# A hybrid encoder step: the sample's place in the order of layer 0's attention tiles

## The chip, the cores and the metric

The kernel runs on one core of a Trainium2 chip. The metric is the device time of one execution in microseconds, taken as the median of several runs. A core has a matrix engine (TensorE, PE in the profile, with its weight loads as PEld), three engines for elementwise work (VectorE, DVE; ScalarE, ACT; GpSimd, POOL), and a queue engine (SyncE, SP) that here only issues DMAs. Each engine executes its instructions in order; semaphores make it wait for others. DMAs are issued from the queues of SP, POOL and ACT.

## What is computed

One inference step of a two-layer encoder, for a prompt of 2048 tokens and a sample group of 32 tokens that share the weights. Layer 0 joins a pooling mixer and a sliding-window attention, layer 1 is a forgetting attention. Cut to layer 0's attention, with q, k, v and the gate from one input projection:

```python
def sink_attention(q, k, v, bias, sinks):
    s = einsum('...qgrd,...kgd->...grqk', q, k) * ATTN_SCALE + bias
    m = maximum(max(s), sink)
    p = exp(s - m)
    w = p / (sum(p) + exp(sink - m))
    return einsum('...grqk,...kgd->...qgrd', w, v)
# prompt: 64-token chunks see themselves and the two chunks before
# sample: 32 tokens see 128 cached keys and their own 32
mixed = concatenate([pool_out, attn]) * silu(gate)
x = x + mixed @ w_out          # for the prompt and for the sample alike
```

Neither group reads anything of the other's, so their order is free.

## The kernel before

The kernel is written in Tile: pools hand out buffers by tag, instructions get their semaphores from a scheduler that also interleaves independent work on each engine. It runs five stages one after another: layer 0's input projection and pooling mixer (which writes q, k, v, the gates and the mixer's values to DRAM), layer 0's attention and output projection, layer 1's input projection with the sample's forgetting attention, the prompt's forgetting attention, and the output projection of layer 1.

Products of fp32 precision are made from exact high and low parts, so an output projection of a 128-token tile takes 8 blocks of the contraction times 3 products times 2 halves, 48 products of 512 columns (L577), and the sample's takes 32, because its high and low parts are stacked in one operand (L582).

The change touches the second stage. It handles 17 token tiles: 16 of the prompt (0 to 15, 128 tokens each) and the sample (number NT = 16, 32 tokens). Each goes through five steps, and the steps of successive tiles are staggered: in turn n the loop calls the load of the n-th tile in `order`, the scores of the one before it, the values of the one before that, then the output projection and the norm of the two before those.

- `stage_load` loads a prompt tile's keys (kk, L623 and L625), values (v2, L627) and queries (qs, L629) by DMAs of POOL's queue, with three buffers for keys and queries. For the sample it loads nothing: keys, values and queries (kabs, v2s, qss) have been prepared in SBUF at the end of stage one.
- `stage_scores` makes two products per head (L653, L654) into one of two PSUM buffers (ps), the bias and the minimum on DVE (L655), the exponential on ACT (L658), and the normalization on DVE (L665).
- `stage_values` loads the gates (sg, L671) and the mixer's values (mp, L673, one buffer) on SP's queue, splits mp into high and low parts on POOL (L157, L158; the first half of the output projection's contraction), transposes the probabilities (L690), multiplies them with the values (L694, L695), joins the halves (L699 to L702), gates on POOL (L703) and splits the result on ACT and DVE (the second half of the contraction).
- `stage_out` loads the residual on SP's queue and calls `out_proj`; for the sample that takes two copies on ACT (L586) and two additions on POOL (L587) besides.
- `stage_norm` makes layer 1's normalized input, transposes it (L725) and stores it.

In turn 2 the eight blocks of the output weights are loaded, four on POOL's queue and four on SP's (L564), and split on ACT and DVE. Turns 0 to 2 get a higher scheduling priority. The order of the tiles is one line, with the sample at the front:

```python
order = [NT] + list(range(NT))
```

SBUF of the first stage is handed to the second buffer by buffer, so most loads of the second stage can begin only when the last products of the first have read their operands. The buffers of one tag are taken in the order in which the code asks for them.

Of the kernel before, what the change touches and what calls it, by code (L numbers as in the profile page):

```python
# [17 lines left out]
P = 128  # L18
# [24 lines left out]
def hybrid_step_kernel(ctx: ExitStack, tc: tile.TileContext, *args):  # L43
# [93 lines left out]
    def rstd_bits(ss, np_, count):  # L137
        """as rstd_of, for one column and without a table: a first guess from the exponent's bits, then Newton"""
# [26 lines left out]
    def flush(n=0):  # L165
        """issue the stores that wait, but for the last n"""
        while len(pending) > n:
            dst, src, eng = pending.pop(0)
            eng.dma_start(dst, src)

    # ------------------------------------------------------------------
    # one layer's input projection, h^T held as exact hi/lo parts
    # ------------------------------------------------------------------
    class Proj:
# [13 lines left out]
        def at(self, which, tok, n):  # L188
            """hi (0) or lo (1) part of h^T for tokens [tok, tok + n): [P, KT, n]"""
# [59 lines left out]
        def prefetch(self, plan, fast=False):  # L249
            """the column groups in the order of use; the next one's weights are loaded ahead"""  # L250
# [49 lines left out]
        def turns(self, new=None):  # L300
            """the turn that waits, one step behind the arithmetic it needs"""
            for f in self.late:
                f()
            self.late = [new] if new else []

        def head_norm(self, src, np_, nh, gB, eng):
            """src: [np, nh, 64] (PSUM or SBUF) -> normalized, scaled tile [np, nh, 64]"""
# [13 lines left out]
    def turn(pt, ev, o, t0, h0, npair, dstT):  # L321
        """normalized heads [P, 2 token tiles, npair x 2 heads x 64] -> exact hi / lo parts, transposed"""
# [11 lines left out]
    # ------------------------------------------------------------------  # L334
    # layer 0, input projection and pooling mixer
    # ------------------------------------------------------------------
    smp_es = ExitStack()

    with ExitStack() as es:
# [91 lines left out]
        # ALiBi with the chunk mask, keys = 128 before the tile and its own 128  # L431
# [11 lines left out]
        # the sample's keys, values and queries for the sliding window, hi / lo parts  # L443
# [114 lines left out]
    # ------------------------------------------------------------------  # L558
    # output projection weights, as exact hi/lo parts
    # ------------------------------------------------------------------  # L560
# [6 lines left out]
    def out_proj(pp, pool, lhs, wo, xres, dst, n, eng):  # L567
        """lhs: for 128 tokens (hi, lo) APs [P, KT, 128]; for the sample one AP [P, KT, 64]"""
# [22 lines left out]
    # ------------------------------------------------------------------  # L591
    # layer 0, sliding-window attention and output projection
    # ------------------------------------------------------------------
    with ExitStack() as es:
# [136 lines left out]
        order = [NT] + list(range(NT))  # L731
# [17 lines left out]
    # ------------------------------------------------------------------  # L749
    # layer 1, input projection  # L750
    # ------------------------------------------------------------------
    late = ctx.enter_context(pool_of(name="late", bufs=1))
    mhs = late.tile([P, KT, 2 * NS], F32R, name="mhs", tag="mhs")
    with ExitStack() as es:
# [38 lines left out]
        # log forget gates and their running sums  # L793
        with pool_of(name="lf", bufs=1) as lf:
# [28 lines left out]
            def running_sums(src_h, nt, dst, tag):  # L823
                """src_h: [P, 16, nt] with positions t*128+p; dst: DRAM [16*nt, 128]"""
# [63 lines left out]
        # forgetting attention of the sample group, one pair of heads  # L888
# [11 lines left out]
        def sample_pair(hp):  # L900
            """generator: both heads side by side, the queries block diagonal"""
# [70 lines left out]
        for gc in range(4):  # L972
            if gc:
                whi, wlo = pj.next_weights()
            for tch in range(NTC):
                for cc in range(2):
# [3 lines left out]
                    # twice the gate, x * (1 + tanh(x / 2)); the half comes in with the softmax's sums  # L980
# [20 lines left out]
    # ------------------------------------------------------------------  # L1001
    # layer 1, forgetting attention over the prompt
    # ------------------------------------------------------------------
# [252 lines left out]
```

## Time and profile before

| | |
|---|---|
| time, median of 3 runs | 2679.44 us (2678.52 to 2679.57) |
| profiled execution, first to last instruction (span) | 2675.6 us |
| profiled execution, its own time outside the span | not shown |
| PE busy | 2586.7 us, 97% |
| DVE busy | 1604.6 us, 60% |
| ACT busy | 1166.4 us, 44% |
| POOL busy | 1149.9 us, 43% |
| DMA, whole span | 126 GB/s in the mean |

The profile is one execution. Its page gives sums over the span and a picture in 40 slices; the trace behind it gives single instructions with start, length, the idle time before them and what ended it. An instruction's length overlaps with its successor's on PE, so the spacing of starts is what a product costs in a full stretch. The granted clock is the share of TensorE's full 2.4 GHz that it got; 0.50 is 1.2 GHz. The attention stage runs from about 480 to about 817 us of the span.

### The profile page before, as it was taken

The numbers are of one execution on the slowest core, as the hardware profiler recorded it, in microseconds if no ns is written. First come the engines' busy times: TensorE is split into PE (matmuls) and PEld (weight loads), VectorE is DVE, ScalarE is ACT, GpSimd is POOL, SyncE is SP. The second block draws the span as 40 slices with busy tenths as digits, with TensorE's granted clock in tenths as the row PEclk, the third lists the DMA queues.
The fourth block names the chain that finished last, engine by engine and source line by source line (L and its number), as shares of the span: only waits on it lengthen the run. The fifth ranks groups of instructions, "written<-read, shape, count | busy, mean of one in ns | idle before, by whom it ended". The sixth has DMA issues, their size and how long they took to land. (4 is left out here: it accounts for less than half of the span.)

```text
span 2675.6 us, 47345 instructions
## 1 busy us (share of the span) xinstructions
PE 2586.7 (97%) x17259; PEld 2345.5 (88%) x17259; DVE 1604.6 (60%) x3847; ACT 1166.4 (44%) x2424; POOL 1149.9 (43%) x1583
## 2 busy tenths in 40 slices
PE   6999999799998999999999999999999999999999
PEld 6999999688887999999999998887888878877787
DVE  7650244778765115554553324889988988888521
ACT  5321111556554122222222114777777777777310
POOL 4454240455534434554554422555555555553100
PEclk9999999799998999999999999999999999999999
DMA  6342110976738443445555316544354455443642
GB/s 187 101 110 88 44 47 23 211 185 169 181 100 266 161 159 97 105 111 132 144 146 139 94 62 162 145 113 122 97 148 120 102 120 141 111 103 90 194 149 75
DMA packets 314120, 338.14 MB, mean 126 GB/s; under 512 B 32311, under 2 KB 263887, under 8 KB 313886
## 3 DMA queue, kind: packets, MB, share of 16 engines
q1 hardware_dynamic: 233550, 242.82, 31.6%
q0 software_dynamic: 76320, 87.98, 15.1%
q10 hardware_dynamic: 4016, 4.31, 0.5%
q8 instruction: 136, 2.23, 0.4%
q14 instruction: 98, 0.80, 0.1%
HBM read 203.05 MB, written 132.06 MB: 125 GB/s over the span
## 5 line engine op out<-in xcount | busy, mean ns | idle before, releaser
L271 PE MATMUL pm<-whl,h 128*128 128x256 f32 (+1 forms) x5760 | 713.7, 283 | 6.3 <-ACT h L155 3.1
L271 PEld LDWEIGHTS pm<-whl,h 128*128 128x128 f32 x5760 | 694.9, 190 | 7.9 <-ACT h L155 3.5
L296 PE MATMUL pm<-h,whl 128*128 128x384 f32 (+2 forms) x2880 | 472.3, 322 | 0.0
L296 PEld LDWEIGHTS pm<-h,whl 128*128 128x128 f32 x2880 | 455.3, 188 | 1.8
L158 POOL TENSOR_TENSOR pl<-pf,ph 128x512 fp32r<-128x512 f32 (+3 forms) x270 | 303.6, 1127 | 263.5 <-DVE ph L157 253.2
L1058 ACT ACTIVATE pr<-pr,mnf 128x128 f32<-128x128 f32 (+15 forms) x256 | 309.6, 1211 | 61.6 <-DVE mnf L1053 60.6
L1077 PE MATMUL pt<-ident,pr 128*128 128x128 f32 x2176 | 323.3, 274 | 5.5 <-DVE pl L158 5.4
L1077 PEld LDWEIGHTS pt<-ident,pr 128*128 128x128 f32 x2176 | 251.2, 141 | 39.3 <-DVE pl L158 11.4
L158 DVE TENSOR_TENSOR pl<-pt,ph 128x512 fp32r<-128x512 f32 (+3 forms) x436 | 261.4, 612 | 39.8 <-ACT ph L155 36.7
L1048 PE MATMUL ps<-ka,qs 128*128 128x512 f32 (+3 forms) x640 | 253.6, 397 | 16.9 <-DVE mnf L1053 15.9
L1053 DVE CUSTOM_DVE_ANT_0 pr<-ps,cb 128x1024 f32<-128x1024 f32 (+7 forms) x256 | 248.8, 981 | 17.9 <-PE ps L1049 9.2
L155 ACT CAST ph<-pt 128x512 fp32r<-128x512 f32 (+3 forms) x436 | 224.9, 529 | 60.9 <-PE pt L1077 44.0
L1070 PE MATMUL pa<-pl,vhl 128*128 128x512 f32 (+3 forms) x640 | 249.2, 395 | 2.3 <-POOL pl L158 2.3
L1070 PE MATMUL pa<-ph,vhl 128*128 128x512 f32 (+3 forms) x640 | 243.6, 383 | 3.8 <-DVE ph L157 3.2
L1049 PE MATMUL ps<-kb,qs 128*128 128x512 f32 (+3 forms) x640 | 228.8, 366 | 0.0
L1082 ACT COPY pf<-pt 128x512 f32<-128x512 f32 (+3 forms) x270 | 140.3, 523 | 66.9 <-PE pt L1077 63.9
L157 DVE CAST ph<-pf 128x512 fp32r<-128x512 f32 (+3 forms) x270 | 143.9, 537 | 35.8 <-ACT pf L1082 35.7
L577 PE MATMUL po<-wo,mh 128*128 128x512 f32 x512 | 162.9, 398 | 0.8 <-ACT mh L155 0.5
L1048 PEld LDWEIGHTS ps<-ka,qs 128*128 128x128 f32 x640 | 121.2, 189 | 46.5 <-DVE mnf L1053 30.3
L157 POOL CAST whl<-wst 128x256 fp32r<-128x256 f32 (+1 forms) x184 | 73.3, 420 | 186.3 <-PE pm L281 105.5
L242 POOL TENSOR_SCALAR wst<-wst,g1c 128x256 f32<-128x256 f32 (+1 forms) x120 | 115.5, 968 | 88.2 <-DMA wst<-in_w_in_dram 86.4
L311 DVE TENSOR_REDUCE ssh<-sq 128x8 f32<-128x512 f32 (+3 forms) x99 | 62.4, 630 | 137.3 <-ACT sq L309 137.2
(396 smaller groups left out, 4050.9 us busy)
## 6 DMA issues: line engine op xcount, KB each, us to landing
qT<-qhl SPq DMA_DIRECT2D x192, 128.0 KB, 2.4
qs<-qT POOLq DMA_DIRECT2D x48, 512.0 KB, 7.3
wst<-in_w_in_dram SPq DMA_DIRECT2D x168, 128.0 KB, 2.6
kT<-qhl SPq DMA_DIRECT2D x128, 128.0 KB, 2.4
ka<-kT POOLq DMA_DIRECT2D x32, 512.0 KB, 7.1
kb<-kT POOLq DMA_DIRECT2D x64, 256.0 KB, 9.0
cb<-cT SPq DMA_DIRECT2D x32, 512.0 KB, 9.6
vhl<-vH POOLq DMA_DIRECT2D x32, 512.0 KB, 4.7
```

Of the source, the lines that this page charges most:

```text
L155: nc.scalar.copy(hi, src)
L157: eng_hi.tensor_copy(hi, src)
L158: eng_lo.tensor_tensor(out=lo, in0=src, in1=f32(hi), op=ALU.subtract)
L271: nc.tensor.matmul(ps[:, j, :], a[:, kt, :], b[:, kt, :], start=(i == 0), stop=(i == 3 * KT - 1))
L296: nc.tensor.matmul(ps, a[:, kt, c:c + P], b[:, kt, :], start=(i == 0), stop=(i == 3 * KT - 1))
L577: nc.tensor.matmul(ps, a[:, kt, :], wo[kt][:, b, cs], start=(i == 0), stop=(i == 3 * KT - 1))
L1048: nc.tensor.matmul(ps[:, s0:s0 + m], lhs, ka[:, ks], start=True, stop=False)
L1049: nc.tensor.matmul(ps[:, s0:s0 + m], lhs, kb[:, ks], start=False, stop=not diag)
L1053: nc.vector.tensor_tensor_reduce(out=pr[:, c0:c0 + n], in0=ps[:, :n], in1=cb[:, :n], scale=1.0, scalar=mns[-1][:, 0:1] if mns else 3e38, o ...
L1058: nc.scalar.activation(pr[:, :L], pr[:, :L], AF.Exp, bias=mns[-1][:, 0:1], scale=-1.0, accum_out=sm)
L1070: nc.tensor.matmul(pa[:, r0 * P:], vhl[b], pp[:, r0:].rearrange("p r q -> p (r q)"), start=(b == 0 and i == 0), stop=(b == nkb - 1 and i = ...
L1077: nc.tensor.transpose(pt[:, r, :], prs[r][:, b * P:(b + 1) * P], ident)
```

## The change

The sample's tile goes from the first place of the order to the ninth, between prompt tiles 7 and 8. Nothing else of the program changes (the rest of the diff takes out comments and docstrings and is left out here).

```diff
@@ layer 0, sliding-window attention and output projection
         tl = {}
-        order = [NT] + list(range(NT))
+        order = list(range(NT // 2)) + [NT] + list(range(NT // 2, NT))
         stages = (stage_load, stage_scores, stage_values, stage_out, stage_norm)
```

The loop over turns is the same. Turns 0 to 2, with the higher priority, now hold the loads of tiles 0, 1 and 2, the scores of 0 and 1, the values of 0 and the output weights; before they held the loads of tiles 0 and 1, the scores of the sample and of 0, the values of the sample and the weights. The sample's instructions on every engine, and its DMAs on SP's queue (gates, mixer values, residual in; residual and norm out), come behind those of tile 7's corresponding turn.

## Rows read from the trace of the kernel before

**Rows 1.** Page, part 2: PE busy in tenths and granted clock, 40 slices.

```profile
PE   6999999799998999999999999999999999999999
...
PEclk9999999799998999999999999999999999999999
```

**Rows 2.** Table by stretches, the saturated one; columns are named in its header.

```profile
core 0: us, PE busy (x) PEld busy (x) DVE busy (x) ACT busy (x) POOL busy (x), PEclk, DMA share, GB/s
...
526.00:790.00 264.00, 259.86 (x1390) 217.58 (x1389) 205.41 (x591) 151.15 (x422) 124.45 (x280) 0.99 0.61 159
```

**Rows 3.** Table by stretches, the start of the attention stage; same columns.

```profile
480.00:484.00 4.00, 1.81 (x11) 1.09 (x11) 3.25 (x17) 1.94 (x4) 3.80 (x7) 0.97 0.81 236
484.00:496.00 12.00, 2.47 (x14) 1.46 (x13) 9.56 (x24) 8.33 (x22) 6.58 (x11) 0.50 1.29 338
496.00:514.00 18.00, 14.40 (x55) 11.63 (x56) 14.46 (x54) 12.10 (x40) 7.18 (x12) 0.50 1.60 312
514.00:528.00 14.00, 13.77 (x69) 9.70 (x69) 12.13 (x34) 8.52 (x25) 8.60 (x9) 0.98 1.19 180
```

**Rows 4.** Timeline of PE: start us, us, line, out<-in, count, [idle before <-releaser].

```profile
382.32 0.32 PE L653 MATMUL ps<-kabs,qss 128*32 128x160 f32 x1
382.48 0.23 PE L654 MATMUL ps<-kabs,qss 128*32 128x160 f32 x1
382.55 3.02 PE L296 MATMUL pm<-h,whl 128*128 128x256 f32 x24
...
498.42 0.47 PE L653 MATMUL ps<-kk,qs 128*128 128x128 f32 x1
...
514.76 3.84 PE L582 MATMUL po<-wo,mh 128*64 128x512 f32 x16
518.44 0.39 PE L695 MATMUL pa<-pl,v 128*128 128x512 f32 x1
518.67 3.85 PE L582 MATMUL po<-wo,mh 128*64 128x512 f32 x16
...
522.36 0.27 PE L653 MATMUL ps<-kk,qs 128*128 128x256 f32 x1
...
523.61 0.71 PE L577 MATMUL po<-wo,mh 128*128 128x512 f32 x2
...
526.44 0.39 PE L577 MATMUL po<-wo,ml 128*128 128x512 f32 x1
...
542.78 0.68 PE L725 MATMUL pt<-ident,hn 32*128 32x32 f32 x8
```

**Rows 5.** Timeline of POOL, its queue's DMA issues included; same columns.

```profile
485.26 0.89 POOL L629 DMA_DIRECT2D qs<-qT  x1 [0.34 <-DMA xr<-in_w_out_dram]
...
500.69 0.30 POOL L157 CAST mh<-mp 128x128 fp32r<-128x128 f32 x1
...
520.62 0.65 POOL L157 CAST mh<-mp 128x512 fp32r<-128x512 f32 x1
...
523.63 1.29 POOL L158 TENSOR_TENSOR ml<-mp,mh 128x512 fp32r<-128x512 f32 x1
```

**Rows 6.** Timeline of SP's queue, loads of the pooling half (mp).

```profile
490.90 0.38 SPq L673 DMA_DIRECT2D mp<-m0T  x1
...
510.59 0.38 SPq L673 DMA_DIRECT2D mp<-m0T  x1
```

**Rows 7.** DMA issues (queue, count, KB, us to landing): span, 485.3, 491.4 us.

```profile
qs<-qT POOLq DMA_DIRECT2D x48, 512.0 KB, 7.3
...
qs<-qT POOLq DMA_DIRECT2D x1, 512.0 KB, 10.4
...
qs<-qT POOLq DMA_DIRECT2D x1, 512.0 KB, 15.3
```

**Rows 8.** Timeline of ACT: last weight cast, cast of tile 0's attention half.

```profile
503.27 1.04 ACT L155 CAST wo<-xr 128x1024 fp32r<-128x1024 f32 x1
...
525.52 0.63 ACT L155 CAST mh<-mix 128x512 fp32r<-128x512 f32 x1
```

**Rows 9.** Waits of PE, 526 to 800 us: total us, times, longest us.

```profile
PE pa L694 <- ACT ph L155: 1.7, 3, 0.9
```

## Prediction

> **What bounds the kernel now.** I read the slices of the page first: TensorE (PE) is busy in nearly every slice, and the granted clock dips only in the eighth and the thirteenth (slices of 66.9 us, so 468 to 535 and 803 to 870 us) [rows 1]. The eighth is where the change acts: layer 0's attention begins at 480 us. The table by stretches [rows 2] shows what follows: from 526 to 790 us PE is busy 259.86 of 264 us at clock 0.99, while VectorE (DVE) has 205.41 (78%) and GpSimd (POOL) 124.45. The middle of the attention stage is bound by PE; work added there costs its PE time, and only 4.1 us of idle could swallow some.
>
> The start is the opposite. From 484 to 496 us PE works 2.47 of 12 us, from 496 to 514 14.40 of 18 us, both at clock 0.50, that is at 1.2 instead of 2.4 GHz; before that fall PE had mostly waited, and the clock is back up in the stretch from 514 on, after PE had been nearly always busy [rows 3]. Counting busy time times clock, PE does 1.76 + 1.24 + 7.20 + 13.5 = 23.7 us of full-speed work in the 48 us from 480 to 528: 24.3 us are lost. That loss is what the order of tiles can change; all other PE work is the same before and after.
>
> **The change part by part.** Only the order list moves: the sample (32 tokens) goes from place 0 to place 8. No instruction is added or removed. I sum against the profiled span, 2675.6 us; the median of the timed runs, 2679.44, is 3.84 above it, and I carry that as a constant (the execution's own time outside its span is not shown).
>
> *What arrives in the middle.* The sample's PE work at full speed. Scores: a pair of products takes 0.23 us (382.32 to 382.55, where one pair ran early in a gap of the pooling mixer), eight pairs 1.84. Output projection: 514.76 to 518.44 and 518.67 to 522.36, together 7.37, 0.23 a product. Values: eight products of fewer columns than the scores' (128 against 160), so at most their 0.115 each, 0.9. Transposes: eight of the sample's norm take 0.68 at full clock; sixteen of the values stage are of the like size, 1.36 at most, of which I take 1.2 because the last one's own length counts once. Sum 11.3 us [rows 4]. The norm's own 0.7 already runs in the full stretch and changes nothing. So the middle grows by 11.3 us. Its DVE, ScalarE (ACT) and POOL work is hidden under PE: 1390 PE instructions [rows 2] at 96 per prompt tile (16 for scores, 16 and 8 for values, 48 for the projection, 8 for the norm) make 14.5 tiles in 264 us, 18.2 us a tile, with 14.2 of DVE. In the step where the sample's projection (7.4) stands in for a prompt tile's (48 products at 0.23, 11.0), the cover shrinks to 14.6 against DVE's 14.2. It holds barely; I charge 0.5 us, with 0 and 2 as ends, and if DVE's share were that much larger the stall would be those 2 us.
>
> *What leaves the start.* Of the 11.3 us, two pairs (0.46) ran before 480 already, in a stretch full of PE work, so the stage starts 0.46 earlier. The other 10.8 lie in the 23.7 us of the start; the prompt (and the mixer's rest) has 12.9 of them. They ran while PE had nothing else: tile 0's first score product starts at 498.42 [rows 4], and its queries, issued on POOL's queue at 485.26, needed 10.4 us to land [rows 5, 7], so 495.7. The sample delayed tile 0's scores by 2.7 us at most; the transfers set the rest. The page's typical time for such a load is 7.3 us, so those of the start suffer from each other, and tile 1's queries even take 15.3 us [rows 7]. POOL's and SP's (SyncE) queues keep the output weights and tile loads; the sample brings only small loads there, so no data comes sooner.
>
> *What fills the hole.* Tile 0's output projection. Its first half of the contraction uses the pooling mixer's values, which need no attention. In the kernel before their load stands behind the sample's: SP issues the sample's at 490.90 and tile 0's only at 510.59 [rows 6], because there is one buffer; POOL casts them at 500.69 and 520.62 [rows 5], and the projection starts at 523.61, two microseconds before ACT casts the attention half at 525.52 [rows 4, 8]. After the change tile 0 is first in that queue: cast near 501, remainder near 503 (0.65 and 1.29 us on POOL [rows 5]), and the weights for these rows are split by then (the last of all eight casts is at 503.27 [rows 8]). 24 of 48 products, 5.5 us at full speed, are then ready from 503, some 20 us sooner. The tile's second value product, which stood behind the sample's projection until 518.44, and all that follows it, can come 3.7 us sooner; with the 2.7 from above the attention half is cast near 519. Until then the pooling half and tile 2's scores (1.9 us) are enough to do.
>
> *The sum of the start.* Estimates from the rows above, full-speed work up to 528: 1.0 for the mixer's rest before 484; nothing until 496; 1.7 for tile 0's scores until 503 (16 products, at half clock); 503 to 514 at half clock, 5.0 (offered are 5.5 of projection, 1.9 of tile 1's scores from about 507, 1.6 of tile 0's transposes and values, more than PE can do); 514 to 528 at full clock with 1.5 us of gaps, 12.5. Together 20.2, all for the prompt, which had 12.9: it is 7.3 us ahead. The sum: 11.3 into the middle, 0.5 of stall there, less 7.3, less 0.46, makes +4.0: the span 2679.6, the time 2683.4.
>
> Unknown is when PE's clock rises. Kept at 514, as before, because PE is about as busy from 503 on as it was from 498. Ends: at full clock from 503 all 9.0 offered are done by 514 and the last stretch is full: 1.0 + 1.7 + 9.0 + 13.5 = 25.2, the prompt 12.3 ahead; not before 521, 3.5 less than 7.3.
>
> The Trainium skill (TensorE: Matmul & The Clock Gate, "Why this matters for your kernels") advises against idle gaps of PE between bursts since the clock falls back; it speaks against taking the sample's products out of the start. By it the clock would stay low until tile 0's projection, the case that the first rival below prices from rows; so far the trace agrees, since the clock is at 0.50 from 484 on [rows 3]. The same page ("Back-to-back issue gap") makes a 512-column product cost its columns at 2.4 GHz plus 2.5 ns, 215.8 ns; an estimate by that page is 6.9 us for the sample's 32 products and a middle that grows by 10.8; the trace has 7.37, which I use.
>
> *Waits.* No wait is added, but the sample's instructions now stand in queues among prompt tiles: POOL's two additions to the sample's residual wait for its projection, and POOL's queue holds the loads of later tiles behind them. Those loads are issued about two tiles ahead (36 us) and land in 7.3 to 15.3 us, which hides a wait of a few microseconds; without that lead a late load would cost up to 15 us.
>
> **The rivals.**
>
> *Nothing fills the hole (slower).* If the instruction order puts tile 0's projection behind its scores and values, PE does by 528 only the prompt work that it does now, 12.9, and about 2.2 us pulled forward with tile 0's scores: 11.3 + 1.0 of stall - 2.2 - 0.46 = +9.6, 2689.1; with the clock low until 521, up to 2 more, 2691.1. It decides where less than 5.9 of the 11.3 us come back. For it: the first product on POOL's remainder came 2.8 us after the projection's first, at 526.44 [rows 4], so it hangs on that queue. Against it: the trace shows the projection starting on the pooling half alone.
>
> *The sample fits into gaps (faster).* The good clock end and the middle's 4.1 us of idle filled: 11.3 - 12.3 - 0.46 - 4.1 = -5.6, 2673.9. For it: the idle is there. Against it: the idle lies in pieces of at most 0.9 us, ended by other engines' results [rows 9], which the sample does not bring forward.
>
> *The change does not do what it says.* The sample's operands lie in SBUF, and two of its score pairs ran 100 us ahead of the stage, so the order might hoist it again: 2679.4 within 2 us. Against it: score tiles share two PSUM buffers with the prompt's, and hoisting it ahead of eight tiles would need these in another order than the code's.
>
> **How the numbers follow.** Forecast case (2674.1 to 2684.8): 0.47. Gaps filled, faster: 0.11. Nothing fills the hole, or half of it: 0.34. No real move: 0.08. About 0.2%, 5.4 us, is what a measurement of this kernel can tell from no change: faster 0.11, same 0.55, slower 0.34. The range runs from 2673.9 (the faster rival's end) to 2691.0 (the slower one's).
>
> **What would show it.** Right: tile 0's score products near 496; its projection starting near 503 on the pooling half; PE nearly empty from 484 to 496; the sample's 32 projection products amid prompt tiles at 0.23 us; the stretch to 790 longer by 11 less the start's gain; layer 1 starting 4 us later and the rest unchanged. Wrong: projection not before 515, then slower; weights or queries landing at other times because their queues were reordered; or layer 1's start changing by itself.

## The result, and the profile after

| | before | after |
|---|---|---|
| median of the timed runs | 2678.98 us (4 runs, 2677.03 to 2679.57) | 2698.74 us (4 runs, 2689.89 to 2700.45) |
| ratio to before | | 1.0071, interval 1.0058 to 1.0085 |
| profiled execution, its span | 2679.44, 2675.6 us | 2698.43, 2696.7 us |

The change costs 19.8 us; 4.0 were forecast, and 2691.0 was the top of the range. Of the 21.1 us by which the spans differ, 16.3 lie in layer 0's attention: from the end of the last pooling product to the end of the last tile's projection it takes 322.2 us before and 338.5 after. Another 2.0 are there before the stage begins and 2.9 after it. Both kernels run the same code there, and over the profiled executions of this study the stage began between 481 and 487 us and the part after it, with the sample not last, took 1869 to 1876; so I look for the cause in the stage.

The table by stretches of after, with the columns of [rows 2], answers [rows 2, 3]:

```profile
core 0: us, PE busy (x) PEld busy (x) DVE busy (x) ACT busy (x) POOL busy (x), PEclk, DMA share, GB/s
484.00:496.00 12.00, 0.00 (x0) 0.00 (x0) 5.70 (x6) 4.18 (x4) 7.66 (x12) 0.59 1.22 330
496.00:514.00 18.00, 10.20 (x39) 8.67 (x40) 9.90 (x31) 9.25 (x22) 7.57 (x12) 0.61 1.43 340
514.00:528.00 14.00, 10.63 (x52) 7.91 (x51) 12.55 (x45) 9.79 (x32) 7.27 (x9) 0.85 1.41 219
526.00:790.00 264.00, 256.22 (x1358) 210.52 (x1357) 195.88 (x604) 147.18 (x430) 120.27 (x267) 0.98 0.62 152
```

PE is empty from 484 to 496 as foreseen, but it also works less than before in both stretches that follow: 10.20 against 14.40 us and 10.63 against 13.77. In the full stretch from 526 to 790 it works 256.22 us where it had 259.86, although the sample's products now lie there too [rows 2]. The timeline of PE in after (columns as in [rows 4]) shows more:

```profile
503.75 0.48 PE L653 MATMUL ps<-kk,qs 128*128 128x128 f32 x1 [19.79 <-DMA qs<-qT]
...
506.94 2.02 PE L577 MATMUL po<-wo,mh 128*128 128x512 f32 x4
...
515.41 0.47 PE L577 MATMUL po<-wo,ml 128*128 128x512 f32 x1
...
524.88 1.94 PE L690 MATMUL pt<-ident,pr 128*128 128x128 f32 x8 [1.26 <-DVE pr L665]
...
664.72 0.40 PE L577 MATMUL po<-wo,ml 128*128 128x512 f32 x1
...
666.15 3.85 PE L582 MATMUL po<-wo,mh 128*64 128x512 f32 x16
...
670.31 3.83 PE L582 MATMUL po<-wo,mh 128*64 128x512 f32 x16
...
701.24 0.39 PE L577 MATMUL po<-wo,ml 128*128 128x512 f32 x1
...
822.01 0.39 PE L577 MATMUL po<-wo,ml 128*128 128x512 f32 x1
...
835.69 0.80 PE L271 MATMUL pm<-whl,h 128*128 128x256 f32 x2 [3.09 <-ACT h L155]
```

Tile 0's first score product waits 19.79 us for its queries and starts at 503.75, not at 498.42 [rows 4]. The filler is there: tile 0's projection on the pooling half runs from 506.94, and its 24th product starts at 515.41. Then it is used up, the probabilities of tile 1 are not ready (at 524.88 PE has waited 1.26 us for DVE's L665), and PE runs dry a second time. The same view in stretches of 4 us, of after:

```profile
504.00:508.00 4.00, 3.95 (x15) 3.38 (x16) 2.63 (x13) 3.29 (x13) 1.81 (x2) 0.50 1.16 332
508.00:512.00 4.00, 4.00 (x17) 3.38 (x16) 2.06 (x12) 1.09 (x6) 0.64 (x1) 0.74 1.14 345
512.00:516.00 4.00, 4.00 (x27) 3.57 (x26) 1.75 (x9) 0.89 (x3) 2.21 (x4) 1.00 1.73 305
516.00:520.00 4.00, 3.89 (x18) 2.30 (x16) 3.83 (x14) 3.92 (x14) 1.96 (x3) 1.00 2.14 238
520.00:524.00 4.00, 1.83 (x9) 1.19 (x8) 3.89 (x13) 3.68 (x15) 4.00 (x5) 0.96 0.84 182
524.00:528.00 4.00, 2.91 (x11) 2.50 (x12) 3.93 (x16) 1.30 (x3) 0.08 (x1) 0.50 0.98 185
```

The granted clock is at 1.00 from 512, a little earlier than before, and falls back to 0.50 after the 1.83 busy microseconds of 520 to 524. In the kernel before, the sample's 32 projection products lay just there, from 514.76 to 522.36 [rows 4].

Why the queries come late is in POOL's queue. First the timeline of POOL in the kernel before, up to tile 0's queries (which are in [rows 5]), then the same in after:

```profile
480.20 2.21 POOL L564 DMA_DIRECT2D xr<-in_w_out_dram  x4 [79.69 <-PE pm L538]
482.37 0.75 POOL L623 DMA_DIRECT2D kk<-kT  x1
483.08 1.27 POOL L625 DMA_DIRECT2D kk<-kT  x2
484.27 0.65 POOL L627 DMA_DIRECT2D v<-vH  x1
```

```profile
482.18 2.19 POOL L564 DMA_DIRECT2D xr<-in_w_out_dram  x4 [78.47 <-PE pm L538]
484.35 1.45 POOL L623 DMA_DIRECT2D kk<-kT  x2
485.77 1.25 POOL L625 DMA_DIRECT2D kk<-kT  x2
487.97 0.59 POOL L625 DMA_DIRECT2D kk<-kT  x1 [0.95 <-DMA xr<-in_w_out_dram]
489.30 0.59 POOL L625 DMA_DIRECT2D kk<-kT  x1 [0.74 <-DMA xr<-in_w_out_dram]
490.80 0.57 POOL L627 DMA_DIRECT2D v<-vH  x1 [0.91 <-DMA xr<-in_w_out_dram]
492.59 0.55 POOL L627 DMA_DIRECT2D v<-vH  x1 [1.21 <-DMA xr<-in_w_out_dram]
493.13 0.90 POOL L629 DMA_DIRECT2D qs<-qT  x1
```

Before, tile 0's five loads follow the four weight loads at once, and its queries go out 5.1 us after the first weight. After, the loads of tiles 0 and 1 are woven: both tiles' keys, then both values, and tile 0's queries 11.0 us after the first weight. No diff line asks for that. The first three turns of the loop each rewind the priority by 300 (L746). Before, turn 0 was the sample, which loads nothing on this queue, and turn 1 alone held tile 0. After, turns 0 and 1 hold tile 0 and tile 1, and by the queue they were interleaved as equals. Both listings show another thing: POOL's queue stood 79 us behind the buffers of the four weights, and all tile loads stood behind it.

The late queries are not all that tile 0's scores wait for. DVE must read the scores, and its queue in after has all eight weight remainders (L158) ahead of the first read (L655):

```profile
503.32 1.23 DVE L158 TENSOR_TENSOR wo<-xr,wo 128x1024 fp32r<-128x1024 f32 x1 [0.38 <-ACT wo L155]
504.47 0.35 DVE L655 CUSTOM_DVE_ANT_0 pr<-ps,bias,nsink 128x128 f32<-128x128 f32 x1
```

With that queue, earlier queries alone could hardly have brought the read forward.

### The profile page after: what moved, and what is told of

It reads as the page before. It is cut to its first block, busy times and chain, and to the rows that moved or that the text cites. A ratio compares the mean times of both kernels' runs of the same rounds, so it can differ in the third digit from the quotient of the medians.

```text
span 2696.7 us, 47329 instructions
## 1 busy us (share of the span) xinstructions
PE 2589.2 (96%) x17259; PEld 2345.9 (87%) x17259; DVE 1599.7 (59%) x3847; ACT 1163.8 (43%) x2424; POOL 1150.5 (43%) x1583
## 5 line engine op out<-in xcount | busy, mean ns | idle before, releaser
L158 POOL TENSOR_TENSOR pl<-pf,ph 128x512 fp32r<-128x512 f32 (+3 forms) x270 | 303.9, 1128 | 281.7 <-DVE ph L157 271.6
L1077 PEld LDWEIGHTS pt<-ident,pr 128*128 128x128 f32 x2176 | 251.3, 141 | 41.4 <-DVE pl L158 11.7
L158 DVE TENSOR_TENSOR pl<-pt,ph 128x512 fp32r<-128x512 f32 (+3 forms) x436 | 261.5, 613 | 41.4 <-ACT ph L155 38.4
L1048 PE MATMUL ps<-ka,qs 128*128 128x512 f32 (+3 forms) x640 | 253.3, 396 | 16.4 <-DVE mnf L1053 15.8
L1053 DVE CUSTOM_DVE_ANT_0 pr<-ps,cb 128x1024 f32<-128x1024 f32 (+7 forms) x256 | 249.1, 982 | 17.8 <-PE ps L1049 11.3
L577 PE MATMUL po<-wo,mh 128*128 128x512 f32 x512 | 163.1, 400 | 1.6 <-DVE xr L588 0.8
```

The source lines that it names most:

```text
L158: eng_lo.tensor_tensor(out=lo, in0=src, in1=f32(hi), op=ALU.subtract)
L577: nc.tensor.matmul(ps, a[:, kt, :], wo[kt][:, b, cs], start=(i == 0), stop=(i == 3 * KT - 1))
L1048: nc.tensor.matmul(ps[:, s0:s0 + m], lhs, ka[:, ks], start=True, stop=False)
L1053: nc.vector.tensor_tensor_reduce(out=pr[:, c0:c0 + n], in0=ps[:, :n], in1=cb[:, :n], scale=1.0, scalar=mns[-1][:, 0:1] if mns else 3e38, o ...
L1077: nc.tensor.transpose(pt[:, r, :], prs[r][:, b * P:(b + 1) * P], ident)
```

## The experiments

My theory after the traces: (a) the sample costs what was forecast in the middle, (b) the woven loads cost several microseconds, (c) the start gives nothing back. The rival: the order of the loads hardly matters, and the sample in the middle costs more than its PE work.

### The order of the loads, restored and imposed

Changed kernel, turn 0 a rank ahead:

```diff
-            with tc.high_priority(offset=300) if n < 3 else nullcontext():
+            with tc.high_priority(offset=400 if n == 0 else 300) if n < 3 else nullcontext():
```

> The changed order, with one difference: turn 0 (tile 0's loads) is rewound by 400 instead of 300, so that POOL's queue has tile 0's keys, values and queries as one block ahead of tile 1's. Theory 'load order' (the two loads, tied in priority, were woven into each other, and tile 0's queries were issued 7.9 us later than before): queries issued near 485 us, first score product near 498 instead of 503.75, and the time 5 to 8 us below the changed kernel's 2698.7, so 2691 to 2694. Rival 'place alone' (the empty start comes from the sample's missing work and the loads' own speed, and the order of the loads hardly matters): within 2 us of 2698.7.

Measured 2691.26 us (2690.78 to 2692.59), 1.0055 of before (1.0038 to 1.0072). The median is 7.5 us below after's, but after's interval, 1.0058 to 1.0085, overlaps with this one, so the pair leaves the size open. Tile 0's loads go first again and its first score comes 12.4 us after the last pooling product, not 19.8. DVE's first read of it comes only 1.5 us sooner, 19.0 us after that product instead of 20.5: six of the eight weight remainders still stand ahead of it. Some 12 us stay, close to the price that the slower rival had. The same order imposed on the kernel before:

```diff
...
+        for t in (0, 1):
+            with tc.high_priority(offset=300):
+                tl[t] = stage_load(t)
         for n in range(NT + 1 + 4):
```

> The kernel before, with the sample in front, but tile 0's and tile 1's loads rewound to the same rank, so that POOL's queue weaves them as in the changed kernel. Theory 'load order': tile 0's queries issued near 493 instead of 485.3, first score product near 504 instead of 498.4, and 4 to 7 us slower than before, 2683 to 2686 (a little less than in the changed order, since the sample's products fill part of the hole). Rival 'place alone': the sample's work covers the later queries, and the time stays within 2 us of 2679.

Measured 2681.19 us (2679.65 to 2685.84), 1.0015 (1.0005 to 1.0024): 2 us where I expected 4 to 7, though tile 0's first score fell to 508.66. With the sample in front PE has other work meanwhile; that this is why so little is lost was not tested apart. So (b) is worth 2 us here, and in the changed order its size is not shown.

### The sample's price in each place

Kernel before without the sample's attention and output projection, and the changed kernel without them:

```diff
         def stage_scores(o):
+            if o.t == NT:
+                return
...
```

> The kernel before without the sample's attention and output projection in layer 0 (its residual is stored and normed as it is loaded; the sample's output is therefore another one). It prices the sample's work in the front. By the prediction it lay beside an empty start: of its 11.3 us of PE work only what delayed tile 0 comes back, 2 to 5 us, so 2674 to 2677. Rival: the front is bound by the sample too and gives the whole 11 us back, 2668.

> The changed kernel without the sample's attention and output projection in layer 0 (as in the run before it). It prices the sample's work in the middle. By the prediction's term it is 11.3 us of PE work and 0.5 of stall: 2698.7 less 11.8, 2686.9. By the ends of the tiles' projections in the two traces (the lag grew by some 14 us across the sample) there is 2 to 3 us of stall more: 2684 to 2685. Its start has the woven loads, so it stays above the run without the sample and with the order of before by the price of these, 5 to 8 us.

Without it, before takes 2677.55 us (2673.94 to 2680.03), ratio 0.9996 (0.9986 to 1.0005), and after 2687.02 (2684.1 to 2690.02), ratio 1.004 (1.0025 to 1.0055). By these medians the sample's own work costs 11.7 us in the middle and 1.3 in front, where it could as well be nothing (in the two profiled executions the stage is 5.0 longer with it). Between the two kernels without a sample lie 9.5 us. That 11.7 - 1.3 + 9.5 is the whole difference follows from how the three are formed and confirms nothing.

I had expected the 9.5 to be the price of the woven loads, which would lie in the start. The traces put it elsewhere. PE and the rest (columns as in [rows 2]) in the kernel before without the sample, then in the changed kernel without it:

```profile
484.00:600.00 116.00, 93.40 (x473) 76.11 (x474) 85.75 (x254) 66.42 (x185) 60.76 (x115) 0.88 0.96 220
600.00:700.00 100.00, 99.18 (x532) 83.12 (x531) 75.02 (x237) 57.87 (x165) 50.43 (x114) 1.00 0.71 177
```

```profile
484.00:600.00 116.00, 93.74 (x473) 77.84 (x474) 84.76 (x250) 65.29 (x180) 58.17 (x109) 0.87 0.92 215
600.00:700.00 100.00, 92.21 (x473) 74.31 (x472) 71.04 (x214) 53.88 (x154) 47.16 (x102) 0.98 0.69 167
```

By 600 us both have done 473 products, so the woven loads have cost nothing there. The second falls behind by 59 products between 600 and 700, and that is where the sample's turn, now without work, stands in its order. PE waits there 7.5 us in many short waits for ACT and DVE, against 0.6 in the first kernel.

The ends of the tiles' projections (the last of a tile's 48 products L577) say the same for all kernels. Times are in us from the end of the last pooling product, one execution each:

| kernel | tile 1 | tile 7 | tile 8 | tile 15 | from 7 to 8 | from 7 to 15 |
|---|---|---|---|---|---|---|
| before | 74.1 | 183.5 | 202.4 | 322.2 | 18.9 | 138.7 |
| after | 70.1 | 181.2 | 217.7 | 338.5 | 36.5 | 157.3 |
| tile 0 a rank ahead | 72.5 | 179.8 | 216.2 | 333.7 | 36.4 | 153.9 |
| before, no sample | 71.2 | 179.3 | 196.0 | 317.2 | 16.6 | 137.9 |
| after, no sample | 69.6 | 180.5 | 209.4 | 326.6 | 28.9 | 146.1 |

The products that end tiles 7 and 8 in after stand above (664.72 and 701.24); in the kernel before they are:

```profile
665.10 0.39 PE L577 MATMUL po<-wo,ml 128*128 128x512 f32 x1
...
683.97 0.39 PE L577 MATMUL po<-wo,ml 128*128 128x512 f32 x1
```

Up to the end of tile 7 after is 2.3 us ahead of before. From there on it loses 18.6 (157.3 against 138.7), 17.6 of them in the step across the sample's place. That is more than the 11.7 that the sample's work is worth: with the work taken out its turn stays, and the tiles behind tile 7 still take some 8 us longer than without a turn in the middle (146.1 against 137.9). The order of the loads moves the end of tile 7 by little more than 1 us, with the sample and without. So the rival holds as far as the traces go: in the middle the sample costs more than its PE work, and the order of the loads hardly shows. Why a turn with little or no work costs so much is argued and not shown: I take it that fewer tiles are then in flight to cover one another's waits for ACT and DVE.

### What keeps the start from giving more back

In the kernel with tile 0 a rank ahead its loads are early again, yet tile 7 ends only 3.7 us sooner than before, where 7.8 were forecast. Its PE, DVE and ACT, in this order:

```profile
498.92 0.45 PE L653 MATMUL ps<-kk,qs 128*128 128x128 f32 x1 [12.43 <-DMA qs<-qT]
...
505.83 0.48 PE L653 MATMUL ps<-kk,qs 128*128 128x128 f32 x1 [5.83 <-DVE mn L655]
```

```profile
502.33 1.23 DVE L158 TENSOR_TENSOR wo<-xr,wo 128x1024 fp32r<-128x1024 f32 x1 [5.07 <-ACT wo L155]
504.28 1.23 DVE L158 TENSOR_TENSOR wo<-xr,wo 128x1024 fp32r<-128x1024 f32 x1 [0.72 <-ACT wo L155]
505.43 0.35 DVE L655 CUSTOM_DVE_ANT_0 pr<-ps,bias,nsink 128x128 f32<-128x128 f32 x1
```

```profile
501.25 1.04 ACT L155 CAST wo<-xr 128x1024 fp32r<-128x1024 f32 x1 [5.25 <-DMA xr<-in_w_out_dram]
```

PE stops after the four score products of two heads and goes on only when DVE has read the first of them (L655). DVE stands behind two weight remainders (L158); these wait for ACT's cast, and that for the weight's transfer. The read itself takes 0.35 us. To see whether these splits are the cause, the same kernel and the kernel before with one weight load in place of eight, split eight times:

```diff
-            st = wl.tile([P, D], F32, name="xr", tag="xr")
-            (nc.gpsimd if kt < 4 else nc.sync).dma_start(st, w[kt * P:(kt + 1) * P, :])
+            if kt == 0:
+                st = wl.tile([P, D], F32, name="xr", tag="xr")
+                nc.gpsimd.dma_start(st, w[0:P, :])
```

> The changed order with tile 0's loads first (as in the first run), but only one of the eight 512 KB row blocks of the output weights is loaded; it is split eight times, so the casts stay and seven transfers (3.5 of 13.4 MB in the start) are left out, and the output is another one. Theory 'transfers bound the start' (the hole the sample leaves is not filled because tile 0's loads, the weights and the splits behind them come at the rate of the DMA): the stall of 5.8 us in tile 0's scores goes, the first score product comes some 5 us sooner, the filling that the prediction counted on (7.3 us) takes place; 8 to 14 us below the 2691.3 of the first run, 2677 to 2683, and only 2 to 6 us above its partner below. Rival 'PE's own order' (the products stand in a queue in an order that leaves the hole, whatever the loads do): within 3 us of 2691, and 12 us above the partner.

> The kernel before with the same seven weight loads left out (one block split eight times; the output is another one). Theory 'transfers bound the start': 4 to 8 us faster than before, 2671 to 2675, less than the gain of its partner, since the sample's work already lies beside the transfers. Rival: within 2 us of 2679.

Measured 2685.41 us (2682.97 to 2689.64), ratio 1.0026 (1.0016 to 1.0036), 5.9 less than with eight loads where I expected 8 to 14, and for before 2679.61 (2678.28 to 2684.04), ratio 1.0004 (0.9995 to 1.0014): no change where I expected 4 to 8. The wait of 5.83 shrinks to 1.24, and tile 7 ends at 173.4 instead of 179.8, so this gain does lie in the start. The weights' transfers hold the start of the changed order and not that of the old one.

### The weights on another queue

The changed kernel with tile 0 a rank ahead, its first four weights issued on ACT's queue, so that POOL's is free for the tile loads:

```diff
-            (nc.gpsimd if kt < 4 else nc.sync).dma_start(st, w[kt * P:(kt + 1) * P, :])
+            (nc.scalar if kt < 4 else nc.sync).dma_start(st, w[kt * P:(kt + 1) * P, :])
```

> The changed order with tile 0's loads first, and the first four output weight loads on ACT's queue. DVE's and ACT's queues then hold two of the eight weight splits behind tile 0's first scores instead of ahead of them, and POOL begins with tile 0's loads. Theory 'queues' (the hole is not filled because tile 0's scores stand behind weight splits that wait for their transfers, a stall of 5.8 us in the first run): the stall shrinks to under 2 us and the time to 2685 to 2688. Rival 'the transfers' total': tile 0's queries or the weights come later for it, and the time stays within 2 us of 2691.

Measured 2686.67 us (2682.63 to 2691.15), ratio 1.0031 (1.0019 to 1.0043), 4.6 less than without, with intervals that overlap a little. Its PE and DVE:

```profile
482.86 0.22 PE L653 MATMUL ps<-kk,qs 128*128 128x128 f32 x1
...
496.56 0.47 PE L653 MATMUL ps<-kk,qs 128*128 128x128 f32 x1 [13.14 <-DVE mn L655]
```

```profile
495.01 1.22 DVE L158 TENSOR_TENSOR wo<-xr,wo 128x1024 fp32r<-128x1024 f32 x1 [0.20 <-ACT wo L155]
496.15 0.34 DVE L655 CUSTOM_DVE_ANT_0 pr<-ps,bias,nsink 128x128 f32<-128x128 f32 x1
```

Tile 0's operands are now there before the stage starts (first score at 482.86, 0.16 before the last pooling product ends), and still the fifth product waits 13.14 us, for a read that stands behind six weight remainders in DVE's queue. Even so tile 7 ends at 168.2, 11.6 us sooner than with the weights on POOL; from there to tile 15 it takes 157.0, as long as in after. The Trainium skill (DMA: Bandwidth & Descriptors, "Issuing engines are not separate DMA queues") says that issuing on several engines saves only the issuing time, which is usually small. Here it also saved the tile loads a wait of 79 us behind the weights in one queue, so the trace differs.

On the kernel before, three other ways for the weights: the same edit; all eight on SP's queue; and six buffers for four (the residuals share them).

> The kernel before with the first four output weight loads issued from ACT's queue instead of POOL's, so that POOL's queue begins with tile 0's loads, about 2.2 us sooner, and the weights are not put off as they were when SP had all eight. If the sample covers what happens until tile 0's queries land (as the run without the sample and the one with a single weight load say), nothing changes: 2677 to 2681. If the first score product sets the start, it comes near 496 and the time is 2 to 3 us lower, 2676 to 2677.

> The kernel before with all eight output weight loads on SP's queue, so that POOL's queue begins with tile 0's keys, values and queries, some 2.2 us sooner (the time of four issues). If tile 0's queries are what the start waits for: first score product near 495 instead of 498.4 and 2 to 4 us faster than before, 2675 to 2677. If the total of the transfers is what the start waits for: no change, within 2 us, or later weights and slower by up to 4 us.

> The kernel before with six instead of four buffers for the output weights and residuals, so that the fifth and sixth weight loads need not wait for the first splits (SP issued them at 487.4). If the weights are hidden behind the sample's work in the order of before: within 2 us of 2679. If they hold DVE and ACT up: 2 to 4 us faster. If they now take the transfers' time from tile 0's queries: 2 to 5 us slower.

Measured 2683.71 us, ratio 1.0023; 2685.99, 1.0027; and 2691.33 (2691.11 to 2693.48), 1.0053. All are slower. In the first two tile 0's loads go out early, from 439 us on, but between 480 and 560 PE waits 8.4 and 7.3 us for DVE's scaled probabilities (L665). With six buffers tile 0's queries are issued at 490.72 instead of 485.26 and its scores begin only at 506.78; PE waits 9.0 us for the sample's L665 and 4.9 for POOL's remainders. In the old order neither earlier tile loads nor more room for the weights is worth anything alone.

### The weights behind tile 0's queries

If the order of DVE's queue holds the start, the weights must come after tile 0's scores. A column copied from tile 0's queries into each weight buffer makes its load wait for them; first in the kernel with the weights on ACT, then in the kernel before:

```diff
+            if kt < 4:
+                nc.scalar.copy(st[:, 0:1], after)
-            (nc.gpsimd if kt < 4 else nc.sync).dma_start(st, w[kt * P:(kt + 1) * P, :])
+            (nc.scalar if kt < 4 else nc.sync).dma_start(st, w[kt * P:(kt + 1) * P, :])
...
+                load_out_weights(wo, wx, w_out0, f32(tl[0].qs[:, 0, 0:1]))
```

> The changed order with tile 0's loads first and the first four weight loads on ACT's queue, the splits on ACT and DVE as in the changed kernel. New: before each of these four loads ACT copies one column of tile 0's queries into the weights' buffer, so that the weights cannot start before the queries are there; all of tile 0's score work then stands ahead of the first split in DVE's and ACT's queues. Theory 'splits ahead of the scores': the wait of 13 us (the run with the weights on ACT) goes, without the two new costs of the run with the splits on POOL (DVE's and POOL's operations side by side, and the last weights issued as late as 536), and the prompt fills the hole: 2674 to 2682. Rival 'weights': the splits, now behind the scores, hold the projection up, and it stays within 3 us of 2686.7.

Measured 2678.14 us (2676.0 to 2683.74, 11 runs), 1.0002 of before (0.9993 to 1.0011): 20.6 below after, 13.1 below the kernel with tile 0 ahead, 8.5 below the one with the weights on ACT. DVE, PE and the stretches of its trace (its lines from L566 on are two higher than before's, so L657 is DVE's read, L667 its scaling and L692 the transposes):

```profile
489.21 0.35 DVE L657 CUSTOM_DVE_ANT_0 pr<-ps,bias,nsink 128x128 f32<-128x128 f32 x1
...
492.49 2.19 DVE L158 TENSOR_TENSOR wo<-xr,wo 128x1024 fp32r<-128x1024 f32 x1 [2.92 <-ACT wo L155]
```

```profile
497.56 1.97 PE L692 MATMUL pt<-ident,pr 128*128 128x128 f32 x8 [7.14 <-DVE pr L667]
```

```profile
484.00:496.00 12.00, 4.60 (x21) 3.62 (x19) 6.80 (x23) 7.98 (x25) 5.22 (x7) 0.61 0.91 266
496.00:514.00 18.00, 13.98 (x49) 10.89 (x50) 15.98 (x37) 11.54 (x26) 1.28 (x1) 0.69 0.96 242
514.00:528.00 14.00, 13.62 (x70) 11.18 (x69) 10.59 (x33) 5.77 (x19) 6.36 (x10) 1.00 0.74 196
```

The queries of tiles 0 to 2 are out by 456, all 16 score products of tile 0 are read before the first weight remainder (489.21 against 492.49), and 484 to 528 now holds 32.2 busy microseconds with no sample in it, against 20.8 in after. The start can be filled, and by more than I forecast: tile 7 ends at 167.6, 15.9 us sooner than before.

But with the weights on ACT alone it ended at 168.2. So the 8.5 us between these two medians (5.9 between the stages of the two profiled executions) do not lie in the start: from tile 7 to tile 15 it takes 151.7 us instead of 157.0, which is 13.0 more than before and hardly more than the sample's own work. What makes the sample's place cheaper here was not tested. PE no longer waits 13.14 us for DVE's first reads, but it waits 7.14 for DVE's scaling, which now stands behind three remainders. That the order of DVE's queue is worth those 8.5 us is not shown.

> The same edit on the order of before, the sample in front (tile 0's loads are whole there anyhow). If the start's loss comes from the splits ahead of the scores and from POOL's queue standing behind the weights' buffers, tile 0's and the sample's work both fit in it: 5 to 12 us faster than before, 2667 to 2674, and 5 to 11 us faster than its partner, the price of the sample in the middle less what the prompt can fill. If only the sample can fill the start: within 3 us of 2679.

In the kernel before, the same edit misses what I expected: 2685.92 us (2683.86 to 2689.44), 1.003 (1.0019 to 1.0042). ACT's queue has the sample's casts in front of the copies, so the first weight is issued only at 493.36 and tile 0's projection starts at 532.57 instead of 523.61. I read the gap of 7.8 us to its partner as the price of that place in the queue; the old order with the copies elsewhere was not measured. No kernel of this study that does all the work beats the one before.

### The splits on POOL, and other places for the sample

Taking the splits off DVE and ACT looked like a way too: four of the eight on POOL with the weights on ACT, in the changed order with tile 0 a rank ahead and in the old one (there with an offset of 500 for turn 1, which loads tile 0).

```diff
...
-            split(wo[kt][:, 0], wo[kt][:, 1], st, nc.scalar, nc.vector)
+            split(wo[kt][:, 0], wo[kt][:, 1], st, *((nc.gpsimd, nc.gpsimd) if kt < 4 else (nc.scalar, nc.vector)))
```

> The changed order with tile 0's loads first and the first four weight loads on ACT's queue (as in the run before), and now the first four of the eight weight splits on POOL; the other four stay on ACT and DVE, behind the scores of tiles 0 and 1 in their queues. Theory 'splits ahead of the scores' (in the run before, tile 0's first scores were ready at 483 but DVE read them at 496, behind six splits that waited for weights): the wait of 13.1 us goes, tile 0's scores run from 483 on, and the hole fills as the prediction had it or better, 7 to 12 us of prompt work: 2674 to 2681, where the run before had 2686.7. Rival 'the hole cannot be filled without the sample, the weights come too late for it': within 3 us of 2687.

> The same three edits on the order of before, with the sample in front. If the splits ahead of the scores cost the start there too, the sample's and tile 0's work both fit into the 24 us that the start loses, and the kernel is faster than before by 5 to 12 us, 2667 to 2674, and faster than its partner with the sample in the middle by 5 to 11. If the sample alone fills what can be filled, it stays within 3 us of 2679.

Measured 2726.68 us (2723.61 to 2730.37), 1.0179, and 2715.2 (2712.8 to 2715.58), 1.0132: clear misses. All of tile 0's scores were done by 494.9, but SP's last weight loads went out only between 499.50 and 536.76, because POOL held their buffers, and PE waited 20.1 us for L665 between 480 and 580. DVE's operations take longer beside POOL's long ones: its timeline in this changed kernel, and in the kernel before:

```profile
497.36 8.08 DVE L665 TENSOR_SCALAR pr<-pr,sm 128x128 f32<-128x128 f32 x8
```

```profile
509.39 2.24 DVE L665 TENSOR_SCALAR pr<-pr,sm 128x128 f32<-128x128 f32 x8
```

Two more orders of tiles: sample second in the kernel before, and sample last in the kernel with tile 0 ahead.

```diff
-        order = [NT] + list(range(NT))
+        order = [0, NT] + list(range(1, NT))
```

> The kernel before with the sample in place 1, between tiles 0 and 1; tile 1's loads are then issued behind the weights again and not woven with tile 0's, and tile 0's pooling values come first through their one buffer. Theory 'what counts is whether the sample lies beside the start's transfers, and tile 0's loads whole': the sample still fills the hole, within 4 us of before, 2675 to 2683. Rival 'the sample must be in front, since only it needs no load' : its scores now stand behind tile 0's in PE's and DVE's queues, so PE is empty until 496 as without the sample and the sample's 11 us come later: 2685 to 2691.

```diff
-        order = list(range(NT // 2)) + [NT] + list(range(NT // 2, NT))
+        order = list(range(NT + 1))
```

> The sample in the last place, with tile 0's loads whole as in the first run. Theory 'the sample's PE time costs its full length wherever tiles keep PE busy, and only a stretch in which PE waits for data hides it': the end of the stage has such a stretch, 13 us between the last projection product and layer 1's first product, but layer 1's loads start there too, and the sample's scores and values lie among the last tiles. Between 2682 (projection and transposes hidden, 8 us of the 12 regained) and 2691 (nothing hidden, as in the middle). Rival 'its place costs more still, since layer 1 waits for the sample's norm at the end': 2692 to 2700.

Measured 2689.49 us (2686.14 to 2692.8), 1.0042, and 2687.52 (2684.81 to 2688.49), 1.0037 (1.0024 to 1.005), 3.7 below the median with the sample in the middle, with intervals that overlap. As second tile it comes too late: PE is empty until 495.62, waits 6.0 us for DVE, and the sample's projection starts only at 530.80. In front the sample hides best, and there it alone needs no load. As the last tile it leaves the step from tile 7 to tile 8 at 18.9 us, as in before, and part of its work lies beside the waits before layer 1, where PE stands 7.39 us for the norm.

## Why the prediction was wrong

*"11.3 into the middle, 0.5 of stall there": mis-sized, the larger step that failed.* The products cost what I took: the projection's take 3.85 and 3.83 us for 16, against 3.84 and 3.85 [rows 4], and taking the sample's work out of after gave 11.7, against 11.8. But that run keeps the sample's turn. From the end of tile 7 to the end of tile 15 after takes 18.6 us longer than before, 17.6 of them in the step across the sample's place; an empty turn there alone costs some 8. I asked only whether DVE is covered in the one step where the sample's projection replaces a tile's, and gave the short waits for ACT and DVE around that place no term.

*"7.3 us ahead" and the two score pairs, 7.8 in all: mis-sized, the other step.* In after tile 1 ends 4.0 us sooner than before and tile 7 only 2.3. Tile 0's first score even came sooner than forecast where its loads kept their order: without the sample 12.1 us after the last pooling product, with it 16.4, so 4.3 us for my 2.7. The filler was named rightly, and "the weights for these rows are split by then" held; but I let the scores, the filler and the values of tiles 0 to 2 run as PE was free and did not ask where their readers stand in DVE's and ACT's queues. With tile 0's loads restored they stand behind weight remainders, and PE waits 5.83 us there; with seven of the eight weight loads left out tile 7 ends 6.4 us sooner, with the weights on ACT 11.6. My sum of the start also ended at 528, as if work done early were never missed later: the filler was used up by 516 and PE ran dry at 520, where the sample's projection had been.

By the tiles' ends the two terms account for the stage: 2.3 us ahead at tile 7, 18.6 lost from there on, together the 16.3 by which it is longer.

*"POOL's and SP's queues keep the output weights and tile loads … so no data comes sooner": wrong too, at a price that is not shown.* It reckoned with data coming sooner or not, and not with data coming later. The change leaves each load on its queue, but moves tile 0 and tile 1 into turns of equal rank, and the queue weaves them. Tile 0's queries, due by 495.7 in my working, released its scores at 503.75. "Queries landing at other times because their queues were reordered" was on my list of what would make the prediction wrong, with no chance and no price; the order that a turn without loads had given to the queue could have been read from L746 and L728 to L744. Measured: 2 us on the kernel before; on the changed kernel 7.5 between medians whose intervals overlap, and little more than 1 of it by tile 7.

*The rivals.* "Nothing fills the hole" has nearly the price of the kernel with restored loads (2691.26; it said 2689.1 to 2691.1), though not its mechanism: the filler ran, and most was lost across the sample's place. Even without the reordered loads it would have beaten my likeliest case. "The sample fits into gaps" and "does not do what it says" fell: the sample's scores start at 628.94, its projection stands between those of tiles 7 and 8, from 666.15 to 674.14, and its products cost their time.

*The signs.* PE empty from 484 to 496: seen (0.00). Projection on the pooling half near 503: seen, at 506.94. Scores near 496: 503.75. Layer 1 four microseconds later: 18.2 (817.46 to 835.69), of which 16.3 belong to the stage.

*What stays open.* Why a turn with little or no work in the middle of the tiles costs 7 to 8 us beyond that work in these kernels, and hardly anything in the one with the weights behind the queries; what the order of the loads is worth in the changed order; and whether a start with tile 0's queries early and the sample in front would beat the kernel before. The tiles' ends come from one execution of each kernel.

## What to carry to other kernels

To price a place in a staggered loop of tiles, compare the step across that place before and after. Leaving the work out prices the work and keeps the turn. When two kernels differ, find first where in the trace they part, by products done or tiles ended, and name the cause then: loads that visibly changed at the start need not be it, and differences that add up by construction prove nothing. An estimate that fills a hole of one engine must follow each filler through the in-order queues of the engines that read its result, and go on until the borrowed work would have been due.

## What the runs showed of the hardware

A queue that issues transfers stops at the first one whose buffer isn't free: POOL's stood 79.69 us behind the weights' buffers, with tile loads behind them whose data were ready. With the weights behind the queries and on ACT's queue those of tile 0 went out from 439.6 to 449.2 instead of 482.4 to 486.2.

DVE's eight scalings of 128x128 took 8.08 us while POOL ran two remainders of 128x1024, 2.4 us each, between its loads, and 2.24 where POOL issued loads and ran one remainder of 128x128, 0.49 us. The Trainium skill (SBUF — State Buffer, "Who interferes with whom") says that DVE and GpSimd share a port pair under an exclusive lock; the trace agrees in kind, with 8.08 against 2.24.

PE's clock fell twice in after: it was at 0.50 (1.2 GHz) when PE started at 503.75 after 20 us of nothing, at 1.00 (2.4 GHz) by 512 after 8 busy microseconds, and at 0.50 again from 524, after a stretch of 4 us with 1.83 busy.
